# Norm and modulation of a two-layer hybrid block: token scaling and high halves moved from VectorE to ScalarE

## The chip, the cores and the metric

The kernel runs on one core of a Trainium2 chip. The metric is the device time of one execution in microseconds, as a median of runs. The core has TensorE (matrix products and transposes, PE in the profile), VectorE (DVE), ScalarE (ACT), GpSimd (POOL) and SyncE (SP), which here only starts transfers; each takes its own list of instructions strictly in order, and they meet through semaphores. TensorE writes to PSUM; VectorE and ScalarE read PSUM, GpSimd does not touch it here.

## What is computed

Two layers of a block over 1024 latent tokens and 256 context tokens of width 1024. Cut to what matters here:

```python
for l in range(DEPTH):
    sh_l, sc_l, gt_l = [m[:, None, :] for m in modulation(c, w_mod[l], b_mod[l])]
    sh_c, sc_c, gt_c = modulation(c_ctx, w_mod[l], b_mod[l])
    h_l = rms_norm(x, g_pre[l]) * (1 + sc_l) + sh_l
    h_c = rms_norm(ctx, g_pre[l]) * (1 + sc_c) + sh_c
    p_l = h_l @ w_in[l]
    p_c = h_c @ w_in[l]
    # four mixers (two attentions, an SSM, a Hyena convolution) over columns of p
    out_l = jnp.concatenate([a_l, g_l, s_l, y_l], axis=-1) @ w_out[l]
    x = x + gt_l * rms_norm(out_l, g_post[l])
    # the context likewise, in layer 0 only
```

The change touches the two lines that make h_l and h_c.

## The kernel before

Each big product is made of float32 values that are split into a rounded high half and a low half (what the rounding left), and three products of halves are added. The input of layer l's projections is kept as two such tiles of 128 x 8 x 1280, `hh` (high halves) and `hl` (low halves): modulated columns, features on partitions, all 1280 tokens along the free dimension.

They are made pair by pair of token tiles of 128 tokens. `xn_tile` (L427) makes the sum of squares of a tile on ScalarE (L430), the reciprocal root with one small VectorE and one small GpSimd instruction (L432), and scales the tile by it on VectorE (L433). `norm_cols` (L435) then goes through the eight feature blocks two at a time: four such steps make a pair. TensorE transposes four 128x128 blocks into one PSUM tile `xps` of 128 x 2 x 256 (L445); each of its two halves is scaled and shifted into an SBUF tile `h`, on ScalarE for the feature blocks 0, 1, 4 and 5 and on VectorE for the others (L448 to L451); VectorE rounds both halves of `h` into `hh` with one cast (L453); GpSimd subtracts to make `hl` (L454). Two `xps` tiles exist at a time.

This happens twice. In layer 0 it stands at the entry, beside the loads, the Hyena filters (`filters`, tiles `hfilt`, `fsb`, `kt`) and the SSM tables (`ssm_poles`, `ssm_tables`, tiles `sE`, `sT`, `sF`, `pww`). For layer 1 it stands in the output projection of layer 0: `outproj` makes a tile of 48 products in PSUM (`ops`), squares it on ScalarE (`oy<-ops`), makes the reciprocal root (`ors`), multiplies by it and the gate on VectorE, adds the old activations on GpSimd, and stores the tile (`xD<-oy`). Then `xn_tile` works on the same tile `y` in place and uses `ops` as the place for the discarded squares; so the PSUM tile is free after that square, and the in-place scaling has to wait until the store has read the tile.

Behind the norm come the projections (`inproj_cols`, products `ipc`, weights `whi` and `wlo`, which ScalarE and GpSimd split), the SSM scan (`sD`, `sV`), Hyena's long convolutions (`hyx`, `lX`, `lU`, last products `lout`), in layer 0 the same for the context (`hcd`, last products `hco`, output tile `hcz`), the SSM's last part (`sglu`), then the gate columns' projections (`ipt`, stored to `gD`), and attention (`aS` are the scores, from keys `kst` and queries `aq`).

The order of the instructions on each engine is not written by hand except in attention: a scheduler places all instructions of the program by priority and by its own idea of their times when the program is built. A change in one instruction can therefore move others far from it.

Of the kernel before, what the change touches and what calls it, by code (L numbers as in the profile page):

```python
# [14 lines left out]
AF = mybir.ActivationFunctionType  # L15
# [172 lines left out]
class K:  # L188
# [238 lines left out]
    def xn_tile(self, P, xt, xn, junk):  # L427

        ss = P.tile([128, 1], F32, tag="ss", name="ss", bufs=3)
        self.act(junk, xt, AF.Square, accum_out=ss)  # L430
        rs = P.tile([128, 1], F32, tag="rs", name="rs", bufs=3)
        self.rsqrt(rs, ss, 1, 1.0 / 1024)  # L432
        self.ts(xn, xt, rs)  # L433

    def norm_cols(self, P, tiles, xns, scl, shf, hh, hl, hb=2):  # L435

        w = 0 if tiles[0] < 8 else 1
        n = 128 * len(tiles)
        c0 = tiles[0] * 128
        for k in range(0, 8, 2):  # L440
            ps = self.b1("xps").rearrange("p (k n) -> p k n", k=2)
            h = P.tile([128, 2, n], F32, tag="h32", name="h32", bufs=hb)
            for j in range(2):
                for q, xn in enumerate(xns):
                    self.tr(ps[:, j, q * 128:(q + 1) * 128], xn[:, (k + j) * 128:(k + j + 1) * 128])  # L445
            for j in range(2):
                a, b = scl[:, k + j, w:w + 1], shf[:, k + j, w:w + 1]
                if k % 4:  # L448
                    self.ts(h[:, j], ps[:, j], a, b)
                else:  # L450
                    self.act(h[:, j], ps[:, j], AF.Identity, scale=a, bias=b)  # L451
            hi = hh[:, k:k + 2, c0:c0 + n]
            self.nc.vector.tensor_copy(hi, h)  # L453
            self.lo(hl[:, k:k + 2, c0:c0 + n], h, hi, self.nc.gpsimd)  # L454


# [1554 lines left out]
```

## Time and profile before

| | us |
|---|---|
| median of 3 runs (2165.46 to 2170.33) | 2168.16 |
| the profiled execution | 2168.31 |
| its span, first to last instruction | 2166.5 |
| TensorE busy | 1933.1 |
| VectorE busy | 1557.0 |
| GpSimd busy | 972.2 |
| ScalarE busy | 896.6 |

The stages in the span are: 0 to some 120 us entry with layer 0's norm; to 716 us projections, SSM and Hyena of layer 0; 737 to 1085 us attention; to 1235 us the output projection with layer 1's norm; to 1779 us the projections, SSM and Hyena of layer 1; to 2085 us attention; then the last output projection. Busy time is to be read stage by stage, since the limiting engine changes. In the tables of stretches a busy time is the union of an engine's instructions in the stretch; the idle time before an instruction is put down to what released it.

### The profile page before, as it was taken

The page shows a single profiled execution, that of the slowest core. Times are in us where ns is not written, and L with a number is a line of the kernel's source. Part 1 is how long each engine was busy: PE and PEld are TensorE (multiplying, and loading weights), DVE is VectorE, ACT ScalarE, POOL GpSimd, SP SyncE. Part 2 cuts the span into 40 slices and gives each one's busy share as a digit, 9 for nine tenths or more (in the row PEclk, how much of TensorE's full clock was granted, in tenths as well). Part 3 has the DMA queues.
Part 4 walks back from the last instruction along what each step waited for, and adds up shares of the span by engine and source line. Part 5 has one row for each costly group of instructions (what it writes and reads, how often), then busy time and mean ns, then how long its engine had stood idle before and what let it go on. Part 6 is the DMA issues. An engine that isn't in the chain of part 4 may idle for free.

```text
span 2166.5 us, 31419 instructions
## 1 busy us (share of the span) xinstructions
PE 1933.1 (89%) x10811; PEld 1602.2 (74%) x10811; DVE 1557.0 (72%) x2969; ACT 896.6 (41%) x1926; POOL 972.2 (45%) x782
## 2 busy tenths in 40 slices
PE   6988998899889599899998898988889979999888
PEld 2677887777768477788777677887766667899766
DVE  5699349757776488788653498479769868999721
ACT  2422234224234367667423222344224227788611
POOL 0757236584461144434156558246566624340034
PEclk9798899899999899999899998999899989999999
DMA  7323365337656545452343423364457675561063
GB/s 254 97 91 136 108 222 142 98 118 239 201 174 197 147 126 154 139 160 80 90 142 123 139 99 130 113 232 137 128 161 223 204 213 142 150 169 46 12 184 126
DMA packets 261280, 316.55 MB, mean 146 GB/s; under 512 B 46671, under 2 KB 203599, under 8 KB 257793
## 3 DMA queue, kind: packets, MB, share of 16 engines
q1 hardware_dynamic: 261120, 314.55, 47.6%
q8 instruction: 85, 1.39, 0.3%
q14 instruction: 75, 0.61, 0.1%
HBM read 207.61 MB, written 106.86 MB: 145 GB/s over the span
## 4 chain that ended last, share of the span: by engine, by line
PE 47%; DVE 29%; DMA 10%; issue 7%; POOL 3%; ACT 2%; SPq 2%; POOLq 0%; DVEq 0%; ACTq 0%
PE ipc L224 9%; PE apo L224 7%; PE apt L253 6%; PE aS L224 6%; PE ops L224 6%; DVE lU L233 3%; DVE sD L233 3%; PE mps L224 2%; SPq L201 2%; DVE sp L233 2%; PE acx L224 2%; PE fdft L224 2%; PE hps L224 1%; DVE lX L233 1%; DVE sV L233 1%
## 5 line engine op out<-in xcount | busy, mean ns | idle before, releaser
L224 PE MATMUL ipc<-hh,whi 128*128 128x512 f32 (+2 forms) x992 | 386.7, 390 | 31.4 <-DVE ipt L236 12.8
L224 PE MATMUL ipc<-hh,wlo 128*128 128x512 f32 (+2 forms) x992 | 381.5, 385 | 3.9 <-POOL wlo L233 3.9
L224 PE MATMUL ipc<-hl,whi 128*128 128x512 f32 (+2 forms) x992 | 382.9, 386 | 0.4 <-POOL hl L233 0.4
L224 PEld LDWEIGHTS ipc<-hh,whi 128*128 128x128 f32 x992 | 196.3, 198 | 65.8 <-DVE ipt L236 15.2
L233 DVE TENSOR_TENSOR aPl<-apt,aPh 128x512 fp32r<-128x512 f32 x328 | 223.8, 683 | 20.7 <-ACT aPh L1672 16.9
L1672 ACT CAST aPh<-apt 128x512 fp32r<-128x512 f32 x328 | 186.5, 590 | 124.2 <-PE apt L253 118.3
L224 PEld LDWEIGHTS ipc<-hh,wlo 128*128 128x128 f32 x992 | 196.5, 198 | 35.2 <-POOL wlo L233 4.6
L224 PEld LDWEIGHTS ipc<-hl,whi 128*128 128x128 f32 x992 | 196.9, 198 | 31.2 <-issue 3.8
L233 POOL TENSOR_TENSOR wlo<-wraw,whi 128x512 fp32r<-128x512 f32 x92 | 139.1, 1516 | 137.1 <-ACT whi L462 103.3
L253 PE MATMUL apt<-ident,aP 128*128 128x128 f32 x1312 | 190.5, 276 | 1.2 <-DVE aPl L233 1.0
L224 PE MATMUL aS<-kst,aq 128*128 128x512 f32 x512 | 152.3, 420 | 26.4 <-DMA aq<-gP 20.8
L1637 DVE TENSOR_REDUCE am<-aS 128x1 f32<-128x1024 f32 x128 | 155.5, 1215 | 21.7 <-PE aS L224 21.6
L246 ACT ACTIVATE aP<-aS,am,rs 128x1024 f32<-128x1024 f32 x128 | 155.5, 1215 | 33.5 <-DVE am L243 32.4
L1700 POOL COPY aLB<-am 128x128 f32<-128x128 f32 x72 | 21.0, 292 | 322.8 <-DVE am L1692 322.8
L253 PEld LDWEIGHTS apt<-ident,aP 128*128 128x128 f32 x1312 | 148.3, 141 | 16.7 <-DVE aPl L233 6.4
L224 PE MATMUL apo<-aPh,vst 128*128 128x256 f32 x656 | 138.3, 308 | 15.3 <-ACT aPh L1672 8.7
L224 PE MATMUL apo<-aPl,vst 128*128 128x256 f32 x656 | 123.5, 286 | 1.6 <-DVE aPl L233 1.3
L224 PEld LDWEIGHTS aS<-kst,aq 128*128 128x128 f32 x512 | 88.2, 192 | 41.7 <-issue 21.2
L224 PEld LDWEIGHTS apo<-aPh,vst 128*128 128x128 f32 x656 | 96.2, 190 | 30.6 <-DVE aob L233 15.8
L224 PE MATMUL ops<-owh,omh 128*128 128x512 f32 x288 | 93.5, 405 | 17.1 <-ACT omh L1785 10.8
L224 PEld LDWEIGHTS apo<-aPl,vst 128*128 128x128 f32 x656 | 100.3, 189 | 8.6 <-DVE aPl L233 3.8
L224 PE MATMUL ops<-owl,omh 128*128 128x512 f32 x288 | 93.3, 404 | 0.0
(369 smaller groups left out, 4382.4 us busy)
## 6 DMA issues: line engine op xcount, KB each, us to landing
wraw<-in_w_col_dram SPq DMA_DIRECT2D x64, 256.0 KB
mraw<-in_w_mod_dram SPq DMA_DIRECT2D x32, 512.0 KB
kst<-mK SPq DMA_DIRECT2D x16, 640.0 KB
omx<-mixD SPq DMA_DIRECT2D x18, 512.0 KB
ogt<-gD SPq DMA_DIRECT2D x18, 512.0 KB
k<-kt SPq DMA_DIRECT2D x16, 512.0 KB
lk<-k SPq DMA_DIRECT2D x8, 1024.0 KB
gD<-ipt SPq DMA_DIRECT2D x32, 256.0 KB
```

Of the source, the lines that this page charges most:

```text
L201: return self.nc.sync.dma_start(out=out, in_=in_)
L224: self.keep(self.nc.tensor.matmul(out, lhsT, rhs, start=start, stop=stop))
L233: self.keep((eng or self.nc.vector).tensor_tensor(out=out, in0=a, in1=b, op=op))
L246: self.keep(self.nc.scalar.activation(out=out, in_=in_, func=func, **k))
L253: self.keep(self.nc.tensor.transpose(out, in_, self.ident[:p, :p]))
L1637: self.keep(nc.vector.tensor_reduce(out=x["m"][:, 2 + qi:3 + qi], in_=x["S"][qi], axis=AX.X, op=ALU.max))
L1672: self.keep(nc.scalar.copy(h, ps))
L1700: self.keep(nc.gpsimd.tensor_copy(x["LB"][:, :, o:o + 64], x["m"][:, 10:12].unsqueeze(2).to_broadcast([128, 2, 64])))
```

## The change

The token tile is scaled by ScalarE in place of VectorE. The high half is no longer a cast of `h` by VectorE: ScalarE makes it straight from the transposed PSUM tile, by the same scale and shift, rounding on the way out. One cast of 128x512 becomes two ScalarE instructions of 128x256. What makes `h` itself stays as it was, and so does GpSimd's subtraction.

```diff
     def xn_tile(self, P, xt, xn, junk):
...
         self.rsqrt(rs, ss, 1, 1.0 / 1024)
-        self.ts(xn, xt, rs)
+        self.act(xn, xt, scale=rs)
...
                     self.tr(ps[:, j, q * 128:(q + 1) * 128], xn[:, (k + j) * 128:(k + j + 1) * 128])
+            hi = hh[:, k:k + 2, c0:c0 + n]
             for j in range(2):
                 a, b = scl[:, k + j, w:w + 1], shf[:, k + j, w:w + 1]
+                self.act(hi[:, j], ps[:, j], AF.Identity, scale=a, bias=b)
                 if k % 4:
                     self.ts(h[:, j], ps[:, j], a, b)
                 else:
                     self.act(h[:, j], ps[:, j], AF.Identity, scale=a, bias=b)
-            hi = hh[:, k:k + 2, c0:c0 + n]
-            self.nc.vector.tensor_copy(hi, h)
             self.lo(hl[:, k:k + 2, c0:c0 + n], h, hi, self.nc.gpsimd)
```

Where VectorE makes `h`, the built program makes the two engines read the PSUM tile in turn: VectorE's instruction waits for ScalarE's on the same half, and ScalarE's on the second half waits for VectorE's on the first. The scheduler also puts the program into another order almost everywhere outside the two attentions. Three places follow.

**End of layer 0's projections, TensorE.** Last products of the context's Hyena branch (`hco`) and first scores (`aS`, `acx`), before:

```order
L224 MATMUL ipc<-hh,whi 128x256
L224 MATMUL ipc<-hl,whi 128x256
L224 MATMUL ipc<-hh,wlo 128x256
L224 MATMUL hco<-hcdi,hcU 128x256 x8
L224 MATMUL aS<-kst,aq 128x512 x4
L224 MATMUL acx<-kst,aq 128x256 x4
```

After, around the same `hco`:

```order
L224 MATMUL ipc<-hh,whi 128x512
L224 MATMUL hco<-hcdi,hcU 128x256 x2
L224 MATMUL ipc<-hl,whi 128x512
L224 MATMUL hco<-hcdi,hcU 128x256 x6
L224 MATMUL ipc<-hh,wlo 128x512
```

From the last row on, 31 projection products of 512 columns and 24 of 256 follow before the first `aS`; before, none did.

SyncE's list at the same place (`owr` and `mraw` are blocks of later weights, `kst`, `vst` and `aq` keys, values and queries), before:

```order
L201 DMA owr<-in_w_out_dram 128x512 x2
L201 DMA mraw<-in_w_mod_dram 128x1024 x2
L201 DMA mixD_77<-hcz_5082 128x256
L201 DMA mraw<-in_w_mod_dram 128x1024
L201 DMA gpre<-in_g_pre_dram 128x8
L201 DMA bmt<-in_b_modT_dram 128x16
L201 DMA mixD_77<-hcz_5090 128x256
L201 DMA kst<-gP_4000 64x2560 x2
L201 DMA vst<-gV_4001 128x10x192
L201 DMA aq<-gP_4000 64x2x256 x6
```

After:

```order
L201 DMA mixD_77<-hcz_5102 128x256
L201 DMA mixD_77<-hcz_5110 128x256
L201 DMA kst<-gP_4020 64x2560
L201 DMA gD_78<-ipt 128x512
L201 DMA kst<-gP_4020 64x2560
L201 DMA vst<-gV_4021 128x10x192
L201 DMA aq<-gP_4020 64x2x256 x5
L201 DMA gD_78<-ipt 128x512
L201 DMA aq<-gP_4020 64x2x256
L201 DMA owr<-in_w_out_dram 128x512 x2
```

The weight blocks moved behind the queries, and two stores of gate columns now stand among keys and queries.

**Output projection, ScalarE.** The tile names are those of the section on the kernel (`ss` and `oss` are the sums of squares), before:

```order
L246 ACTIVATE h_10743<-xps,shf,scl 128x256 x2
L246 ACTIVATE ops,ss<-oy 128x1024
L1785 CAST omh<-omx 128x1024
L246 ACTIVATE oy,oss<-ops 128x1024
L246 ACTIVATE h_10763<-xps,shf,scl 128x256 x2
```

After:

```order
L246 ACTIVATE ops,ss<-oy 128x1024
L1785 CAST omh<-omx 128x1024
L246 ACTIVATE oy,oss<-ops 128x1024
L246 ACTIVATE oy<-oy,rs 128x1024
L246 ACTIVATE hh<-xps,shf,scl 128x256
L246 ACTIVATE h_10763<-xps,shf,scl 128x256
L246 ACTIVATE hh<-xps,shf,scl 128x256
L246 ACTIVATE h_10763<-xps,shf,scl 128x256
```

The scaling (`oy<-oy,rs`) and the high halves (`hh`) now stand between the squares of one tile and the next. At the end of this stage, TensorE's list has 48 projection products between its last `ops` and the last transposes of the norm before, and 63 after.

**End of layer 1's projections, TensorE.** Last products of Hyena (`lout`) and the first scores, before:

```order
L224 MATMUL ipc<-hh,wlo 128x512
L224 MATMUL lout<-hfi,lX 128x128 x12
L224 MATMUL ipc<-hh,whi 128x512
L224 MATMUL ipc<-hl,whi 128x512
L224 MATMUL ipc<-hh,wlo 128x512
L224 MATMUL sglu<-sz,sgw 128x256 x2
```

After:

```order
L224 MATMUL ipc<-hh,wlo 128x512
L224 MATMUL lout<-hfi,lX 128x128 x4
L224 MATMUL sglu<-sz,sgw 128x256 x4
L224 MATMUL lout<-hfi,lX 128x128 x12
L224 MATMUL sglu<-sz,sgw 128x256 x8
L224 MATMUL aS<-kst,aq 128x512 x4
L224 MATMUL sglu<-sz,sgw 128x256 x4
L224 MATMUL acx<-kst,aq 128x256 x4
```

Before, 51 projection products stand between the last `lout` and the first `aS`; after, all of them stand ahead of `lout`.

## Rows read from the trace of the kernel before

**Rows 1.** The page, part 1: busy us, share of span, instructions

```profile
PE 1933.1 (89%) x10811; PEld 1602.2 (74%) x10811; DVE 1557.0 (72%) x2969; ACT 896.6 (41%) x1926; POOL 972.2 (45%) x782
```

**Rows 2.** Table of stretches: length, busy PE, PEld, DVE, ACT, POOL; clock, DMA share, GB/s

```profile
51.00:120.00 69.00, 64.01 (x289) 45.04 (x287) 52.20 (x111) 29.09 (x55) 47.85 (x39) 0.83 0.32 100
120.00:216.00 96.00, 79.09 (x493) 69.42 (x493) 94.73 (x207) 20.57 (x38) 61.34 (x43) 0.89 0.31 112
216.00:716.00 500.00, 456.56 (x2499) 390.65 (x2497) 331.89 (x555) 163.14 (x385) 237.34 (x190) 0.95 0.54 166
716.00:737.00 21.00, 0.23 (x1) 0.26 (x2) 0.42 (x1) 0.00 (x0) 6.67 (x4) 0.62 0.92 237
1085.00:1235.00 150.00, 133.36 (x587) 105.50 (x586) 62.23 (x108) 44.20 (x77) 89.75 (x64) 0.95 0.40 129
1235.00:1755.00 520.00, 463.90 (x2482) 388.56 (x2481) 422.75 (x793) 161.78 (x361) 298.38 (x214) 0.93 0.50 160
1755.00:1779.00 24.00, 19.25 (x74) 15.04 (x73) 9.98 (x25) 6.06 (x15) 0.00 (x0) 0.86 0.93 231
```

**Rows 3.** Groups, ScalarE, 51 to 120: busy us, mean ns; idle before, releasers

```profile
L246 ACT ACTIVATE h<-xps,shf,scl 128x256 f32<-128x256 f32 x20 | 10.2, 560 | 19.2 <-PE xps L253 14.0 <-POOL hl L233 2.9 <-DVE scl L236 2.3
L246 ACT ACTIVATE xn<-xt 128x1024 f32<-128x1024 f32 x7 | 7.3, 1049 | 0.0
```

**Rows 4.** Groups, VectorE, 0 to 216 us: what the change takes away

```profile
L453 DVE CAST hh<-h 128x512 fp32r<-128x512 f32 x20 | 10.1, 530 | 1.7 <-ACT h L246 1.6
L241 DVE TENSOR_SCALAR xn<-xt,rs 128x1024 f32<-128x1024 f32 x10 | 9.0, 909 | 0.6 <-POOL rs L233 0.4
```

**Rows 5.** Groups, VectorE, 1085 to 1235 us: what the change takes away

```profile
L453 DVE CAST hh<-h 128x512 fp32r<-128x512 f32 x20 | 8.8, 484 | 0.3 <-ACT h L246 0.3
L241 DVE TENSOR_SCALAR oy<-oy,rs 128x1024 f32<-128x1024 f32 x10 | 8.7, 868 | 31.8 <-DMA xD<-oy 26.3 <-POOL rs L233 5.6
```

**Rows 6.** Chain that ended last, 51 to 120 us: start, us, what

```profile
53.52 0.67 DVE hh L453 x2
...
118.14 0.34 DVE hh L453
```

**Rows 7.** Timeline, TensorE, end of layer 0's projections: start, us, instruction, [idle before, releaser]

```profile
699.87 0.40 PE L224 MATMUL ipc<-hh,whi 128*128 128x512 f32 x1
700.11 0.39 PE L224 MATMUL ipc<-hl,whi 128*128 128x512 f32 x1
...
711.89 4.07 PE L224 MATMUL hco<-hcdi,hcU 128*128 128x256 f32 x16 [0.32 <-DVE hcU L233]
736.77 2.05 PE L224 MATMUL aS<-kst,aq 128*128 128x512 f32 x4 [20.81 <-DMA aq<-gP]
```

**Rows 8.** Timeline, VectorE, the same place

```profile
722.30 0.42 DVE L233 TENSOR_TENSOR hcz<-hco,hcx 128x256 f32<-128x256 f32 x1 [7.18 <-DMA mixD<-hcz]
```

**Rows 9.** Timeline, SyncE's issues, the same place

```profile
713.95 1.10 SPq L201 DMA_DIRECT2D mraw<-in_w_mod_dram  x2
...
722.75 0.33 SPq L201 DMA_DIRECT2D mixD<-hcz  x1
...
725.07 6.54 SPq L201 DMA_DIRECT2D aq<-gP  x6
```

**Rows 10.** Waits of TensorE, 1085 to 1240 us: us in total, times, longest

```profile
PE ops L224 <- ACT ops L246: 6.3, 3, 4.4
...
PE xps L253 <- DVE ors L243: 3.8, 4, 1.2
```

**Rows 11.** Timeline, TensorE, end of layer 1's projections

```profile
1750.99 3.06 PE L224 MATMUL lout<-hfi,lX 128*128 128x128 f32 x24 [0.28 <-DVE lX L236]
...
1777.85 1.69 PE L224 MATMUL aS<-kst,aq 128*128 128x512 f32 x4 [0.17 <-PE sglu L224]
```

**Rows 12.** Timeline, SyncE's issues, the same place

```profile
1756.15 0.38 SPq L201 DMA_DIRECT2D mixD<-hyt  x1
...
1767.55 1.43 SPq L201 DMA_DIRECT2D aq<-gP  x2
```

## Prediction

> **What bounds the kernel now.** I read the page's sums first: TensorE is busy 89% of the span, VectorE 72%, ScalarE 41% [rows 1]. That says only that ScalarE has room on average, so the second view was the table of stretches [rows 2], and there the stages differ. In the 69 us in which layer 0's norm runs (51 to 120 us) TensorE has 64.0, VectorE 52.2 and ScalarE 29.1 us of work. From 120 to 216 us VectorE is the limit, 94.7 of 96 us, while TensorE stands idle for 17: the SSM tables and the filters are VectorE work, and projections queue behind their products. From 216 us to the end of layer 0's projections TensorE has 456.6 of 500 us; then come 21 us in which no engine works and the DMA share is 0.92. In the output projection (1085 to 1235 us, with layer 1's norm) TensorE has 133.4 of 150 us and VectorE 62.2. So VectorE work is worth its full length only at the entry, and TensorE's idle time is what any gain must come out of: 17 us before 216, 43 from there to 716, 21 at the handover, 17 in the output projection, 56 in layer 1's stretch.
>
> **What is removed and added.** At the entry VectorE loses 20 casts of a high half (10.1 us) and 10 scalings of a token tile (9.0 us) [rows 4]; in the output projection the same again, 8.8 and 8.7 us [rows 5]. ScalarE gets for each cast two reads of half a PSUM tile, as its own modulation of such a half costs today, 0.560 us [rows 3]; for each scaling a pass over 128x1024, which its Square of the same tile prices at 1.049 us [rows 3]. So VectorE gives up 36.6 us and ScalarE takes on 80 x 0.560 + 20 x 1.049 = 65.8 us. The change also adds a wait: where VectorE modulates a half, both engines now read one PSUM tile, and the build lets them do so only in turn (ScalarE, VectorE, ScalarE, VectorE). Behind a ScalarE instruction that waits for such a turn stand squares, filter copies and weight casts of its queue.
>
> **Entry of layer 0.** Best case: of the 19.1 us that VectorE loses here, 16.8 lie after 51 us (three scalings, some 2.3 us, come before), and since VectorE is full until 216 the tables end 16.8 us sooner. Worst case of the plain sum: the chain of work passes through casts and scalings in eight places (the first and the last in [rows 6]), together 4.7 us for eight casts and two scalings; on ScalarE the same ten steps are 8 x 1.12 + 2 x 1.05 = 11.1 us, a loss of 6.4. ScalarE's load between 51 and 120 us rises from 29.1 to 29.1 + 40 x 0.56 + 7 x 1.05 = 58.9 of 69 us, so of the 40 us that it waits there today only 10 would fit. The norm will therefore end later than at 120 us, and VectorE has filter work to fill that with, but not the tables' inputs. I take -2 us, nearer to the middle of -16.8 and +6.4 than to the gain; both ends are kept.
>
> **Handover from layer 0's projections to attention.** The lists of instructions were made anew by the scheduler, and here they differ in TensorE's favour. Before, the last products of the context's Hyena branch (hco) are the last thing that TensorE has before the scores; it then waits 20.8 us for the queries [rows 7]. After, 31 projection matmuls of 512 columns and 24 of 256 stand behind hco. One of 512 takes 0.235 us from start to start [rows 7], one of 256 about half of that as an estimate, so 7.3 + 2.9 = 10.2 us of work moves into the hole. SyncE's list differs too: before, four weight blocks of 256 KB and three of 512 KB stand ahead of the loads of keys and queries, after, they stand behind the first six query loads. VectorE's second output tile there waits 7.2 us for the store of the first one, behind those blocks [rows 8], and the queries are issued only after the second store [rows 9]. If the blocks' absence halves that wait it is 3.6 us more. I take -14 us; the ends are -10.2 (nothing but the cover) and -20.8 (no hole at all). The projections that fill the hole come from earlier places in TensorE's list, so this is a gain only if TensorE has no new wait there.
>
> **Output projection with layer 1's norm.** VectorE's scaling is made in place, so it waits for the store of the unscaled tile, 26.3 us in all [rows 5], and the statistics of the next tile (ors) stand behind it. TensorE feels that as 6.3 us of waiting for a PSUM buffer and 3.8 us for transposes' inputs [rows 10]. On ScalarE the wait for the store stays, but VectorE goes on with the next tile's statistics and its product with the gate. If both TensorE waits go it is -10.1 us. I take -4, since in ScalarE's list the scaling has the next tile's square right behind it in some tiles and ahead of it in others. What comes late next is the last pair of tiles: its last transposes stood behind 48 projection matmuls after the last output product and now stand behind 63, 15 x 0.235 = 3.5 us, and what takes its memory over (the loads of layer 1's table inputs) starts by so much later: +3.5, between 0 and +5.
>
> **Handover to attention in layer 1.** Here the new list is worse. Before, 51 projection matmuls (12.0 us) stand behind the last Hyena product (lout); after, they stand ahead of it, and eight small products are all that TensorE has until the scores. From lout's end (1754.05) to the scores it is 23.8 us now [rows 11]. If that chain keeps its length, the scores start 12 us later. Part of it goes: the loads of the queries are issued 11.4 us after the store of the Hyena output [rows 12], and of what SyncE does between the two, the stores of two gate blocks no longer stand there; I give it 8 us. So +4, between -5 (what TensorE idles there today, 24.0 - 19.25, gone too [rows 2]) and +12.
>
> **The sum.** The profiled execution took 2168.31 us (its span is 2166.5), as good as the median of 2168.16. -2 - 14 - 4 + 3.5 + 4 = -12.5, which gives 2155.8, rounded to 2156 us. The rest of the order changes too (in layer 0 Hyena's first convolution now starts ahead of the SSM scan), and TensorE idles 43 us there and 56 us in layer 1's stretch [rows 2]. No row tells what a new order does to these waits; I take nothing, and about a fifth of each, 8 us and 11 us, either way.
>
> **The rivals.** *VectorE's relief counts in full at the entry* (-16.8 in place of -2): 2141 us. For it: 94.7 of 96 us. Against it: the norm must then not end later, with ScalarE at 58.9 of 69 us. *Given back:* the gain at layer 0's handover is the loss at layer 1's. With -14 there, +12 here, +3.5, and -4 in the output projection it is -2.5, about 2166 us, within 0.2% (4.3 us, about what a measurement of this kernel can tell from no change). For it: the work in the holes is only moved, never removed. *ScalarE's queue paces the output projection:* the 26.3 us of waiting for stores now stand in a queue that also holds the square whose end frees the PSUM tile, and the wait reaches TensorE in full in place of today's 10.1 us: +16 in place of -4, 2176 us, slower. It decides from the point where a scaling ends later than the next tile's products do. For it: the 26.3 us are over twice what one tile's products take TensorE (48 x 0.235 = 11.3 us). Against it: ScalarE is busy 44.2 of 150 us there [rows 2]. The Trainium skill, "ScalarE: Activation LUTs", section "Rules for kernel authors", says that multiplying and adding belong on VectorE and not on ScalarE. By that rule the moved work only gets longer; the rows agree on the price (65.8 for 36.6 us), and where ScalarE is the late one the time would be this rival's.
>
> **How the numbers follow.** Forecast 0.48, with a range of its own of 2147 to 2163; full relief 0.10; given back 0.22; paced by ScalarE 0.20. The prediction is the likeliest case's, 2156 us. The range that should hold the time 8 times in 10 adds the ends of the terms and the unknown order (about 20 us either way) and reaches nearly to the slower rival: 2136 to 2177. Faster by over 0.2%: 0.48 + 0.10 = 0.58. Within: 0.22. Slower: 0.20.
>
> **What would show it.** Entry: VectorE's full stretch should end at about 214 us or sooner; if ScalarE is busy over 90% between 51 and 130 us and the last high half comes after 135, the relief was lost there. First handover: TensorE's wait for the queries at the first scores should be under 10 us. Output projection: no wait of TensorE for the square (ops from ACT) of over 2 us; if there are several, ScalarE paces it. Layer 1's handover: idle time of TensorE between lout and the first scores of 10 to 16 us; over 20 means that the chain kept its length. The prediction is wrong in kind if the time is lost or won between 216 and 716 us or between 1235 and 1755 us, where I put nothing.

## The result and the profile after

The changed kernel is slower: 2192.24 us in the median (2188.17 to 2199.06, 4 runs) against 2169.24 us, a ratio of 1.0113 (95% interval 1.0093 to 1.0133; the intervals below are of the same kind). Forecast was 2156 us, with 2136 to 2177 as the range. Its profiled execution has a span of 2186.4 us, 19.9 longer than that of before. The page, part 1:

```profile
PE 1949.0 (89%) x10811; PEld 1621.2 (74%) x10811; DVE 1529.6 (70%) x2909; ACT 958.7 (44%) x2026; POOL 955.3 (44%) x782
```

VectorE has 27.4 us less and ScalarE 62.1 us more than in [rows 1], where the prediction moved 36.6 and 65.8. But TensorE, with the same 10811 products, is busy 15.9 us longer. The table of stretches, columns as in [rows 2]:

```profile
51.00:120.00 69.00, 61.79 (x339) 45.80 (x339) 43.55 (x93) 53.66 (x99) 42.83 (x38) 0.90 0.31 96
120.00:216.00 96.00, 73.73 (x433) 63.35 (x431) 86.70 (x216) 24.34 (x46) 64.82 (x40) 0.88 0.33 116
216.00:716.00 500.00, 450.85 (x2402) 387.34 (x2403) 324.03 (x522) 158.19 (x373) 228.50 (x192) 0.91 0.52 161
716.00:737.00 21.00, 19.48 (x97) 16.23 (x96) 8.51 (x15) 3.77 (x8) 2.91 (x2) 1.00 0.41 120
1085.00:1235.00 150.00, 138.11 (x616) 109.89 (x615) 49.82 (x73) 73.47 (x126) 88.88 (x64) 0.97 0.43 136
1235.00:1755.00 520.00, 468.46 (x2478) 395.48 (x2477) 402.20 (x779) 162.60 (x360) 281.87 (x208) 0.91 0.51 160
1755.00:1779.00 24.00, 14.17 (x67) 11.93 (x67) 21.69 (x37) 4.90 (x12) 7.84 (x7) 0.79 0.46 147
```

The hole at 716 us is gone (19.48 of 21 us busy, 0.23 before), and the output projection has 616 products where it had 587. In the two long stretches the granted clock is 0.91 (0.95 and 0.93 before), and at 1755 us TensorE has 14.2 us of work where it had 19.3.

A stretch of fixed times mixes progress and order. So I count TensorE's work instead: each product by the time from its start to the next one's in the trace of before (the 20th percentile of its form, that is undisturbed), summed in the order of each trace. The table says how much later than before a run has done the same amount of work (us; from one profiled execution each; the last row is the difference of the spans). The runs e1 to e18 are told below. The table has a noise of its own: a later run, e5, has TensorE's products in the order of the changed kernel up to 1246 us, and its trace stands at 12.2 us at the first scores and 8.0 at the last output product, where that of the changed kernel stands at 8.0 and 1.6. A difference of 4 to 6 us between two traces is no finding.

| when before has done it | after | e1 | e2 | e10 | e13 | e6 | e15 | e17 |
|---|---|---|---|---|---|---|---|---|
| 120 | -3.6 | 16.6 | 1.6 | 18.4 | 5.6 | 0.7 | 0.6 | 0.3 |
| 300 | -1.4 | 16.5 | 8.4 | 18.2 | 4.9 | 1.0 | 0.5 | -0.1 |
| 360 | 21.4 | 15.1 | 31.5 | 17.4 | 3.7 | 4.0 | 0.3 | -1.2 |
| 400 | 12.9 | 16.0 | 23.0 | 18.4 | 4.6 | 8.2 | 1.2 | -0.3 |
| 640 | 16.1 | 13.7 | 25.7 | 18.7 | 4.4 | 4.7 | -0.7 | -4.9 |
| 700 | 24.2 | 13.7 | 34.3 | 18.7 | 4.4 | 7.3 | 1.9 | -0.8 |
| first scores, 737 | 8.0 | 13.6 | 18.3 | 18.6 | 4.2 | -7.3 | -12.6 | -14.9 |
| last output product, 1205 | 1.6 | 12.6 | 10.1 | 18.3 | 2.3 | -16.0 | -21.2 | -20.0 |
| 1260 | 1.0 | 15.6 | 11.0 | 18.3 | 2.4 | -16.1 | -22.4 | -20.4 |
| 1740 | 0.2 | 17.1 | 6.9 | 22.9 | 2.4 | -13.6 | -18.6 | -19.6 |
| 1800 | 18.3 | 16.1 | 23.4 | 23.8 | 1.9 | -12.8 | -18.7 | -19.7 |
| end | 19.9 | 16.7 | 24.7 | 24.8 | 4.8 | -12.0 | -17.0 | -18.2 |

The changed kernel loses 25.6 us between 300 and 700 us, wins 16.2 at the handover and 6.4 in the output projection, is level with before at 1740 us, and loses 18.1 us in the 60 us around layer 1's handover, in a layer in which the change touches nothing. The first loss is not of one place: 22.8 us go between 300 and 360, 8.5 of them are back at 400, and 8.1 go again between 640 and 700, where TensorE is busy for all 60 us before and for 54.0 in the changed kernel. So half of what the handover wins was lost just ahead of it; from 640 us to the first scores the net gain is 8.1.

**Layer 1's handover.** TensorE's waits, 1735 to 1806 us of the changed kernel (us in total, times, longest):

```profile
PE sglu L224 <- DVE sz L236: 9.6, 3, 3.9
PE lout L224 <- DVE lX L233: 7.8, 1, 7.8
PE aS L224 <- DMA sgg<-uD: 5.4, 1, 5.4
```

Its timeline there:

```profile
1768.43 2.08 PE L224 MATMUL lout<-hfi,lX 128*128 128x128 f32 x8 [7.80 <-DVE lX L233]
...
1778.28 1.99 PE L224 MATMUL sglu<-sz,sgw 128*128 128x256 f32 x8 [2.03 <-DVE sz L236]
...
1784.23 3.78 PE L224 MATMUL sglu<-sz,sgw 128*128 128x256 f32 x8 [3.95 <-DVE sz L236]
1793.41 2.05 PE L224 MATMUL aS<-kst,aq 128*128 128x512 f32 x4 [5.40 <-DMA sgg<-uD]
```

The projections that covered this chain before [rows 11] are used up; TensorE waits for each link of it, and eight `sglu` take 3.78 us behind such a wait where the eight before took 1.99.

**From 300 to 360 us.** Stretches of before, then of after (columns as above):

```profile
300.00:360.00 60.00, 52.88 (x321) 49.00 (x320) 55.31 (x93) 29.30 (x71) 30.68 (x35) 0.96 0.67 210
```

```profile
300.00:360.00 60.00, 45.92 (x243) 42.45 (x241) 48.07 (x59) 22.00 (x54) 34.22 (x32) 0.80 0.50 157
```

SyncE's issues, before and after (`ssM` is the last of the SSM tables, `sU` the scan's inputs, `hyx` those of Hyena's first convolution):

```profile
271.21 0.39 SPq L201 DMA_DIRECT2D ssM<-smt  x1
...
274.81 16.75 SPq L201 DMA_DIRECT2D sU<-uD  x32
...
303.62 0.94 SPq L201 DMA_DIRECT2D hyx<-hyD  x2
```

```profile
277.21 1.06 SPq L201 DMA_DIRECT2D hyx<-hyD  x2
278.33 0.43 SPq L201 DMA_DIRECT2D ssM<-smt  x1
...
287.59 18.12 SPq L201 DMA_DIRECT2D sU<-uD  x32
```

The last table leaves 7.1 us later, the scan's loads start 12.8 us later, and Hyena's stand ahead of them instead of behind. Up to 300 us TensorE has projections to do instead (it is busy without a pause from 216 to 300); then it waits for the scan, for Hyena and for the tables (`sy` and `drv` are products of the scan, `set` is a loaded table). Its largest waits from 296 to 362 us, before and after:

```profile
PE sy L224 <- DVE sD L233: 2.8, 4, 1.5
```

```profile
PE sy L224 <- DVE sD L233: 3.9, 1, 3.9
PE lout L224 <- DVE lX L233: 3.5, 1, 3.5
PE drv L224 <- DMA set<-ssE: 3.0, 1, 3.0
```

Which part of the order makes these waits was not taken apart. That Hyena's loads stand in front can't be all of it: e4 below loses 19.8 us in the same 60 us with Hyena's loads behind the scan's, and there TensorE waits 13.0 us for the table.

### The profile page after: what moved, and what is told of

It reads as the page before. It is cut to its first block, busy times and chain, and to the rows that moved or that the text cites. A ratio compares the mean times of both kernels' runs of the same rounds, so it can differ in the third digit from the quotient of the medians.

```text
span 2186.4 us, 31441 instructions
## 1 busy us (share of the span) xinstructions
PE 1949.0 (89%) x10811; PEld 1621.2 (74%) x10811; DVE 1529.6 (70%) x2909; ACT 958.7 (44%) x2026; POOL 955.3 (44%) x782
## 4 chain that ended last, share of the span: by engine, by line
PE 46%; DVE 27%; DMA 10%; issue 7%; SPq 4%; POOL 3%; ACT 3%; POOLq 0%; DVEq 0%; ACTq 0%
PE ipc L224 9%; PE apo L224 6%; PE ops L224 6%; PE aS L224 6%; PE apt L253 6%; SPq L201 4%; DVE sD L233 3%; DVE lU L233 3%; PE mps L224 2%; PE acx L224 2%; PE fdft L224 1%; PE hps L224 1%; DVE aPl L233 1%; DVE sp L233 1%; DMA px<-qkvD 1%
## 5 line engine op out<-in xcount | busy, mean ns | idle before, releaser
L224 PE MATMUL ipc<-hh,whi 128*128 128x512 f32 (+2 forms) x992 | 389.6, 393 | 27.2 <-DVE ipt L236 12.6
L224 PEld LDWEIGHTS ipc<-hh,whi 128*128 128x128 f32 x992 | 198.7, 200 | 64.5 <-DVE ipt L236 15.6
L224 PE MATMUL aS<-kst,aq 128*128 128x512 f32 x512 | 154.4, 424 | 18.2 <-ACT aP L246 7.1
L1637 DVE TENSOR_REDUCE am<-aS 128x1 f32<-128x1024 f32 x128 | 155.6, 1216 | 13.6 <-PE aS L224 13.6
L246 ACT ACTIVATE aP<-aS,am,rs 128x1024 f32<-128x1024 f32 x128 | 155.7, 1216 | 15.6 <-DVE am L243 14.6
L253 PEld LDWEIGHTS apt<-ident,aP 128*128 128x128 f32 x1312 | 149.1, 141 | 16.5 <-DVE aPl L233 7.0
L1700 POOL COPY aLB<-am 128x128 f32<-128x128 f32 x72 | 21.2, 294 | 308.8 <-DVE am L1692 308.8
L224 PEld LDWEIGHTS aS<-kst,aq 128*128 128x128 f32 x512 | 89.3, 195 | 33.4 <-issue 11.9
L224 PE MATMUL ops<-owh,omh 128*128 128x512 f32 x288 | 93.9, 407 | 14.1 <-ACT omh L1785 10.4
L224 PE MATMUL ops<-owh,oml 128*128 128x512 f32 x288 | 92.5, 402 | 0.5 <-POOL oml L233 0.5
```

Source lines behind the costliest of these rows:

```text
L224: self.keep(self.nc.tensor.matmul(out, lhsT, rhs, start=start, stop=stop))
L246: self.keep(self.nc.scalar.activation(out=out, in_=in_, func=func, **k))
L253: self.keep(self.nc.tensor.transpose(out, in_, self.ident[:p, :p]))
L1637: self.keep(nc.vector.tensor_reduce(out=x["m"][:, 2 + qi:3 + qi], in_=x["S"][qi], axis=AX.X, op=ALU.max))
L1700: self.keep(nc.gpsimd.tensor_copy(x["LB"][:, :, o:o + 64], x["m"][:, 10:12].unsqueeze(2).to_broadcast([128, 2, 64])))
```

## Experiments: the work and the order taken apart

The programs differ in two ways, in the work moved and in the order of all other instructions. The next two runs cross them. An order is imposed by edges without a semaphore between consecutive instructions of one engine, taken from the other program's schedule:

```diff
+    for e in ENG:                  # TensorE, VectorE, ScalarE, GpSimd, SyncE
+        both = [keys[k] for k in order[e] if k in keys]
+        for a, b in zip(both, both[1:]):
+            tc.add_manual_dep(b, a.name, ...)
```

**e1**, the change in the old order. 

> The change in full, but every engine issues the instructions that both kernels have in the order of the kernel before; only the 100 new ScalarE instructions find their own places. Theory A (the new order of the rest costs the 23 us): the loss is gone, 2150 to 2172 us. Theory B (the moved work itself is too dear on ScalarE): the loss stays, 2185 to 2198 us. Half and half would be some 2180 us.

**e2**, the old work in the new order. 

> The reverse: the kernel before, with scaling and casts on VectorE, but all other instructions in the order of the changed kernel. Theory A: the loss is here too, 2183 to 2200 us. Theory B: about the time of before, 2165 to 2172 us. If both parts count, the gains of the first run and of this one add up to the 23 us.

| median, ratio to before | old order | new order |
|---|---|---|
| old work | 2168.10 | e2: 2198.33, 1.0134 (1.0116 to 1.0153) |
| moved work | e1: 2190.42, 1.0104 (1.0088 to 1.0119) | after: 2192.24, 1.0113 (1.0093 to 1.0133) |

Both theories are right in one half and wrong in the other. Either change alone costs 22 to 30 us, both together 23, so they don't add up: what the moved work costs depends on the order it stands in. The table of equal work says where. In e1, whose list on TensorE is that of before row by row, the whole loss arises between 51 and 120 us, in the norm, and stays to the end. In e2 and in after, which share a list, 23 us go between 300 and 360 and 16 to 18 around 1770, with either work.

**e3** and **e4**, each part of the change alone, in the scheduler's own order. 

> Only the scaling of the token tiles moves to ScalarE (both places), the high halves stay VectorE casts; the scheduler makes its own order. Theory A: the time is that of one more order, anywhere in 2145 to 2195 us, and this part and the other do not add up to +23. Theory B: the scaling (20 x 1.05 us) is the smaller part, 2170 to 2177 us.

 

> Only the high halves move to ScalarE (80 x 0.56 us), the scaling stays on VectorE; the scheduler makes its own order. Theory A: anywhere in 2145 to 2195 us. Theory B: the larger part of the loss, 2183 to 2192 us, and with the run before it the sum is +23.

Scaling only: 2175.70 us (1.0032, 1.0021 to 1.0042); high halves only: 2183.07 us (1.0067, 1.0054 to 1.0079). Both lie in theory B's ranges (and in A's, which hold nearly anything), and the sum of their losses is near 23 us, as B says, but the traces don't show its reason: by the same count of work e4 loses 19.8 us between 300 and 360 and 12.3 between 1740 and 1800, as e2 does without any moved work, and e3 is 17.6 us ahead of before at 1740 us and then loses 21.9 up to 1800; its longest wait there is again `sglu` on VectorE, 18.0 us in all.

## Experiments: layer 1's order

**e5** and **e6** follow the program's own order up to the last low half of layer 1's norm and the order of before from there: the changed kernel, and the one with only the scaling moved. 

> The change in full, in its own order up to the last low half of layer 1's norm; what is left then (layer 1) in the order of the kernel before. Theory A (layer 1's new order, above all its handover to attention, costs the 18 us that the two traces differ by after 1740 us): 2166 to 2175 us, and the wait at layer 1's first scores is as before. Theory B (layer 1 is late because layer 0's tail is): the loss stays, 2184 to 2195 us.

 

> Only the scaling on ScalarE, in that program's own order up to the last low half of layer 1's norm (where its trace is 17 us ahead of the kernel before), then layer 1 in the order of the kernel before. Theory A: the 17 us are kept, 2150 to 2157 us, faster than both kernels. Theory B: layer 1 gives them back as it did in the program's own order, 2170 to 2178 us.

e5 took 2178.74 us (1.0043, 1.0026 to 1.0059), 13.5 less than the changed kernel; e6 2156.74 us (0.9953, 0.9936 to 0.9971), 19.0 less than e3 and faster than both kernels. e6 is in theory A's range; e5 lies between the two ranges. By the count of work e5's trace loses 1.2 us between 1740 and 1800, where that of the changed kernel loses 18.1, so theory A holds for the place. That the median gains 13.5 and not 18 stays open; e5's profiled execution took 2185 us, 6 above its median. TensorE's waits in e6, 1725 to 1780 us:

```profile
PE sglu L230 <- ACT ipt L252: 4.7, 1, 4.7
PE sglu L230 <- DVE sz L242: 4.6, 1, 4.6
PE lout L230 <- DVE lX L239: 1.2, 2, 1.1
```

## Experiments: what the entry loses in the old order

All in the order of before, with the change at layer 0's entry alone. First the high halves of the feature steps in which ScalarE makes `h` too (e7), then those in which VectorE does (e8), the scaling (e9), and all high halves (e10):

```diff
+            on_act = HI[at] == "A" or HI[at] == ("O" if k % 4 else "E")
             for j in range(2):
+                if on_act:
+                    self.act(hi[:, j], ps[:, j], AF.Identity, scale=a, bias=b)
...
+            if not on_act:
+                self.nc.vector.tensor_copy(hi, h)
```

> In the order of the kernel before, at layer 0's entry alone, and only the high halves of the feature steps in which ScalarE makes h too (20 ScalarE instructions for 10 casts): no two engines read one PSUM tile. Theory T (the turn of the two engines at a PSUM tile makes the norm late): hardly any loss, 2166 to 2173 us. Theory Q (ScalarE's queue is too long in the norm): half of the 17 us or so, 2174 to 2179 us.

 

> The same with the other 10 casts, where VectorE makes h, so that the two engines read the PSUM tile in turn. Theory T: nearly all of the 17 us, 2180 to 2187 us. Theory Q: as much as the run before, 2174 to 2179 us.

 

> In the order of the kernel before, at layer 0's entry alone, and only the ten scalings of token tiles on ScalarE. The two halves of the high halves cost 0 and 5 us. Theory S (the scaling is what is left of the entry's 13.5 to 17 us): 2178 to 2184 us. Theory J (the parts cost little by themselves and pile up in ScalarE's queue only together): 2166 to 2174 us.

 

> The same with all high halves of the entry on ScalarE and the scaling on VectorE. Theory S: the sum of the two runs with half of them, 2172 to 2177 us. Theory J: more than the sum, 2178 to 2185 us.

| | median | ratio |
|---|---|---|
| e7, 10 casts, ScalarE makes h | 2171.29 | 1.0003 (0.9989 to 1.0016) |
| e8, 10 casts, VectorE makes h | 2174.89 | 1.0029 (1.0014 to 1.0044) |
| e9, scaling | 2168.35 | 0.9999 (0.9988 to 1.0011) |
| e10, all 20 casts | 2190.15 | 1.0096 (1.0075 to 1.0117) |

The scaling costs nothing, theory S falls. The halves cost 0, some 5 and 21 us: neither T nor Q said that. J did in kind (more than the sum), though its range for e10 ended at 2185 us. Waits of VectorE, then of TensorE, 51 to 136 us of e10:

```profile
DVE h L249 <- ACT hh L252: 33.7, 17, 5.0
```

```profile
PE xps L259 <- ACT h L252: 11.5, 6, 2.5
```

In e8 the same two waits are 15.7 and 2.1 us, in before the second is 1.3. The longest wait in e10, on VectorE's and on ScalarE's timeline:

```profile
104.63 0.68 DVE L239 TENSOR_TENSOR hfilt<-hps,fdec 128x512 f32<-128x512 f32 x1
110.31 0.55 DVE L249 TENSOR_SCALAR h<-xps,scl,shf 128x256 f32<-128x256 f32 x1 [5.00 <-ACT hh L252]
```

```profile
107.37 0.56 ACT L252 ACTIVATE hh<-xps,shf,scl 128x256 fp32r<-128x256 f32 x1 [3.60 <-PE xps L259]
...
109.18 0.64 ACT L252 ACTIVATE hsq<-hfilt 128x512 f32<-128x512 f32 x1
109.70 1.03 ACT L252 ACTIVATE hh<-xps,shf,scl 128x256 fp32r<-128x256 f32 x2
110.60 0.59 ACT L252 ACTIVATE h<-xps,shf,scl 128x256 f32<-128x256 f32 x1
```

VectorE's `h` reads its tile only after ScalarE's `hh`, and that one stands in ScalarE's list behind the four instructions of the step before, the first of which waited 3.60 us for its tile, and behind a filter's square. Before, the two engines worked on two steps side by side.

**e11** keeps the order of before on TensorE, GpSimd and SyncE alone, with scaling and all high halves of the entry moved. 

> Scaling and all high halves of the entry on ScalarE; TensorE, GpSimd and SyncE keep the order of the kernel before, VectorE's and ScalarE's lists are the scheduler's to arrange anew. If the entry's loss is VectorE's waiting behind ScalarE in a list that was made for other work, it falls to under 7 us: 2166 to 2176 us. If it is the moved work as such: 2179 to 2188 us.

 It took 2182.07 us (1.0068, 1.0048 to 1.0089), in the range for "the moved work as such". Taken alone it would have misled: VectorE still waits 17.2 us for `hh` there.

**e13** is e10 with the two readers turned round:

```diff
-                if on_act:
+                if on_act and not k % 4:
                     self.act(hi[:, j], ps[:, j], AF.Identity, scale=a, bias=b)
                 if k % 4:
                     self.ts(h[:, j], ps[:, j], a, b)
...
+            if on_act and k % 4:
+                for j in range(2):
+                    self.act(hi[:, j], ps[:, j], ...)
```

> As the run with all high halves of the entry on ScalarE (2190 us), but in the feature steps in which VectorE makes h the build lets VectorE read the PSUM tile first and ScalarE after it. Theory W (the loss is VectorE's list standing behind ScalarE's instructions, 33.7 us of waiting there): most of it goes, 2168 to 2178 us. Theory L (all four feature steps of a pair now pass through ScalarE, where two of them had VectorE to themselves, and TensorE waits for PSUM tiles): it stays, 2183 to 2193 us.

 It took 2172.02 us (1.0013, 0.9999 to 1.0026): 18 of the 21 us are gone, with the same 40 instructions on ScalarE. VectorE's longest waits are now for statistics and PSUM tiles:

```profile
DVE rs L249 <- ACT xn L252: 11.0, 6, 4.9
DVE h L249 <- PE xps L259: 8.2, 4, 3.7
```

Theory W is shown for this order: the loss was VectorE's list standing behind ScalarE's.

**e16**, the full change with VectorE first, old order. 

> The change in full at both places, but in the feature steps in which VectorE makes h the build lets VectorE read the PSUM tile first; order of the kernel before. The first run, with ScalarE first, gave 2190 us. If the turn of the two readers is the whole loss of the moved work: 2166 to 2174 us. If the output projection, or scaling and halves together, cost by themselves: 2176 to 2186 us.

 2175.65 us (1.0040, 1.0023 to 1.0056; single runs from 2170 to 2189): 14.8 us of e1's 22 are gone, some 8 remain. What these are was not settled; the result lies between the two ranges, and the profiled execution took 2189 us, 13 above the median, so its trace can't place them.

## Experiments: whose gain is it

**e12** puts the old work into the order of e6. 

> The kernel before, with scaling and casts on VectorE, in the order of the run of 2157 us (that of the program with only the scaling moved, to the end of layer 1's norm, then that of the kernel before). If the gain is the order's alone: 2152 to 2161 us. If it is the scaling's: 2165 us or more; where an order fits only the work it was made for, as the run with the old work in the changed kernel's order says, it is slower than before, 2172 to 2182 us.

 2162.03 us (0.9969, 0.9958 to 0.9980), between the two ranges: at least half of e6's gain is the order's alone.

**e14** and **e15** have only the scaling moved and change orders twice: that of before, from 2353 (e14) or 2000 (e15) of TensorE's instructions on that of e3, and from the end of layer 1's norm that of before again. 

> Only the scaling on ScalarE. The order of the kernel before up to the last Hyena product of layer 0's latent part, from there to the end of layer 1's norm the order of the program with only the scaling moved, then the order of the kernel before. If the 11 us at the first handover and the 9 us in the output projection are gains of those places alone, whatever stands ahead: 2146 to 2153 us. If the handover's gain was work put off earlier, from 300 to 640 us, where that order was 8 to 10 us behind: 2155 to 2166 us.

 

> The same with the first change of order earlier, at the beginning of Hyena's second convolution of layer 0 (2000 of TensorE's 9553 instructions). Gains of the places alone: 2146 to 2154 us. Work put off: it finds more to put off than the run before, 2152 to 2160 us.

 e14: 2157.61 us (0.9945, 0.9930 to 0.9961). e15: 2147.52 us (0.9896, 0.9878 to 0.9914), the fastest of all. e14 lies in the range for work put off, and by the count its trace loses 9.4 us between 640 and 700 and wins 14.9 at the handover, 5.5 net. e15 is in the range for gains of the places alone: in the table it is within 2 us of before up to 700 and wins 14.5 at the handover, 11.9 net of what goes between 640 and 700.

**e17** and **e18** put the old work, and the full change with VectorE first, into the order of e15. 

> The kernel before, with scaling and casts on VectorE, in the order of the run of 2147.5 us. If the 21 us that that run gains are the order's alone: 2145 to 2152 us. If scaling in place on VectorE holds the output projection up, by some 5 us as between the runs of 2157 and 2162 us: 2151 to 2157 us. If an order serves only the work it was made for: 2165 us or more.

 

> The change in full, VectorE first where both read, in the order of the run of 2147.5 us, which has only the scaling moved. If the high halves on ScalarE neither gain nor lose where VectorE is not held up: 2145 to 2152 us. If VectorE's relief at the entry counts (up to the 16.8 us of the prediction): 2131 to 2144 us. If ScalarE's longer queue costs: 2153 us or more.

 e17: 2149.51 us (0.9916, 0.9902 to 0.9931); e18: 2161.41 us (0.9968, 0.9953 to 0.9982). So nearly all of the 21 us are the order's, and an order that was made for another program can serve the old work better than its own (e12, e17). The scaling on ScalarE has a median 5 us lower in the order of e6 (against e12) and 2 lower in that of e15 (against e17); the intervals overlap both times, so neither is shown. e18 is in the range for ScalarE's longer queue: the high halves on ScalarE cost some 14 us against e15 even with VectorE first. Their traces differ by 7.9 us, of which some 7 arise between the first scores and the last output product; in the output projection TensorE there waits 8.2 us for transposes behind ScalarE, in e15 2.6. But this order was made from programs that cast on VectorE, and no run had the high halves in an order made for them that is as good; so it is not shown that they must cost this.

## Why the prediction was wrong, step by step

Two steps failed. The rest of the order was put at nothing, 8 us either way in layer 0; it cost 25.6 us there. And the handover of layer 1, at most +12, cost 18.1, because its chain of work started late. Both losses are there with the old work in the same order (e2). The other terms of the sum came within some 4 us of the forecast in the count of work, which is within its noise, and not all for the reason given.

- **Durations** were near: a high half took 0.567 us (0.560 assumed), the scaling 1.151 (1.049); ScalarE had 53.7 of 69 us in the norm (58.9).
- **Entry, -2.** By TensorE's work at 300 us it is -1.4, but that is luck: TensorE had projections to do while the norm's last low half ended at 133.9 us instead of 120.8 and the last table left 7.1 us later, past my worst end of +6.4. In this order that is not the moved work's doing alone: in e2, with the old work, the last low half ended at 143.5. What I missed of the moved work shows in the old order. I added the durations of the ten steps on the chain and named the turn at the PSUM tile, but looked only at what stands behind the waiting instruction in ScalarE's list, not in VectorE's; there that wait is worth 18 us (e10 against e13). VectorE's waits for it, 51 to 136 us, in e1 and in the changed kernel:

```profile
DVE h L248 <- ACT hh L251: 32.6, 17, 4.6
```

```profile
DVE h L243 <- ACT hh L246: 7.2, 5, 2.3
```

  The turn agrees with a rule that I had not weighed: the Trainium skill, "PSUM — Partial Sum Buffer", section "Terms", says that ScalarE and VectorE must not be on one bank and the same partitions at once, two reads included. All runs here keep the turn, and none shows what happens without it.
- **The reorder elsewhere, 0 with 8 us either way.** This is the term that was mis-sized most: +25.6 from 300 to 700 us, and it is there with the old work too (e2). I had seen Hyena's first convolution move ahead of the scan and took a fifth of TensorE's idle time as the bound. Idle time bounds what can be won there, not what can be lost. That the order is the cause is shown by e2; which of its moves is open.
- **Handover of layer 0, -14.** Measured -16.2; the wait for the queries fell from 20.8 us [rows 7] to 5.6, and e15 and e17 win 14.5 and 14.1 at the same place. Right in place and size, and under the 10 us that I had named as its sign. My condition, no new wait earlier, did not hold: net of the 60 us ahead of it the gain is 8.1. The row after:

```profile
744.78 2.04 PE L224 MATMUL aS<-kst,aq 128*128 128x512 f32 x4 [5.62 <-DMA aq<-gP]
```

- **Output projection, -4.** Measured -6.4 (with attention, which takes the same time in both), little more than the noise of the table, but the reason is not borne out: e2, in the same order with VectorE still scaling, wins 8.2 there. TensorE's waits, after, 1085 to 1240 us; the first of [rows 10] fell to 3.7, and new ones came:

```profile
PE xps L253 <- DVE h L243: 4.0, 2, 2.2
PE ops L224 <- ACT ops L246: 3.7, 3, 2.4
PE xps L253 <- ACT h L246: 2.4, 2, 2.2
```

- **Tail, +3.5.** Measured -0.6, just under the lower end of 0 to +5. The norm's last low half does start 4.3 us later (1236.0 against 1231.7), but TensorE has projections to do.
- **Handover of layer 1, +4.** Measured +18.1, past the +12 of a chain that keeps its length; TensorE waits 7.8, 2.0, 4.0 and 5.4, 19.2 us in sum, between the projections' end and the scores. My sign looked in the wrong place: the 11.4 us behind lout are within the 10 to 16 that I had named, the 7.8 ahead of it were not in it. From lout's end to the scores it is 17.2 us (23.8 before), shorter by 6.6 where I had given it 8, but lout ends at 1776.3 in place of 1754.1. I priced the cover that was lost, but not that the chain itself would start late: the last Hyena products waited 7.8 us for VectorE, and with the holes the clock fell. With the old order it is gone (e5, e6).
- **The rivals.** ScalarE pacing the output projection (2176 us) gave the right sign for the wrong place. One reason for it was misread, too: the 26.3 us are the sum of seven waits, 3.8 us each in the mean, and not to be held against one tile's 11.3. "Given back" had the mechanism at both handovers (-16.2 and +18.1); it lacked the loss after 300 us, which the prediction named as what would make it wrong in kind. The rule that I named from the Trainium skill, "ScalarE: Activation LUTs", section "Rules for kernel authors", that multiplying and adding belong on VectorE, agrees with e18 against e15, as far as that comparison goes, and is not borne out at the entry, neither for the scaling (e9: no difference) nor for the high halves with VectorE first (e13: 1.0013, not clear of 1).

In the 21 us at the first handover GpSimd works for 6.67 us [rows 2]; that no engine works there was misread, and nothing hangs on it.

The sum by the table: -1.4 + 25.6 - 16.2 - 6.4 - 0.6 - 0.8 (1260 to 1740) + 18.1 + 1.6 = 19.9.

## What to carry to other kernels

When a scheduler makes the order, an edit is two changes: cross them, work by order, before either is blamed. Where two engines read one PSUM tile in turn, count what stands behind the waiting instruction on both, and try both turns: here the second one saved 18 us in one order. A handover between stages deserves its own look at the order: here two of them were worth more than the edit, and a better order with the work unchanged beats the kernel before by 18 us (e17).

## What the hardware showed that was not expected

Of the 19.9 us only 4.0 are idle time of TensorE; 15.9 are the same products taking longer. TensorE is busy for 232.8 us at the lower of its two levels (1.2 GHz), where before has 194.3, and 22.5 us less at the upper (2.4 GHz). The granted clock of the trace falls to the lower level, in both places told of above, in or right behind waits of 2 to 8 us: 0.80 is the mean from 300 to 360 us against 0.96, and of two groups of eight `sglu` products (above) the one at the upper level took 1.99 us, the one at the lower, behind the wait of 3.95, 3.78.

One GpSimd instruction of the tables took 8.85 us in the changed kernel, its likes in before 1.47 in the mean, while VectorE ran from 171.3 to 181.1 us without a pause; VectorE's next table then waited 6.74 us for its store. Rows of after, GpSimd and VectorE:

```profile
171.67 8.85 POOL L233 TENSOR_TENSOR sT<-pwt 128x640 f32<-128x640 f32 x1 [1.64 <-DVE pwt L233]
```

```profile
187.81 0.83 DVE L233 TENSOR_TENSOR sT<-pwt 128x640 f32<-128x640 f32 x1 [6.74 <-DMA ssT<-sT]
```

The same is there in two other runs of this order (8.84 in e5, 8.85 in e2). The Trainium skill, "GPSIMD Engine Reference", section "Specifications", says that GpSimd shares its ports to SBUF with VectorE and is in contention with VectorE's instructions of two SBUF inputs; the run of such instructions at that place agrees. No experiment took VectorE's run away, so the cause is argued, not shown.
